# A two-layer transformer block on one Trainium2 core: first feed-forward halved, first products side by side, convolution taps as diagonal matrices on TensorE

## The chip, the core and the metric

The kernel runs on one core of one Trainium2 chip. The time is device microseconds of one execution, from its start to its end, the median of three runs. The engines are TensorE (PE, matmuls; PEld is its weight load, which overlaps them), VectorE (DVE), ScalarE (ACT), GpSimd (POOL) and SyncE (SP), whose queue issues the DMA transfers.

## The reference

Two layers work on 512 tokens x and 256 context tokens (768 rows together) of width 1024. Each layer is a feed-forward, a mixer and a feed-forward, each of them behind an RMS norm that is modulated by a conditioning vector. The even mixer joins latent attention with an mLSTM; the odd mixer is a short convolution with a gated linear recurrence. In the last layer only x is kept.

```python
def modulate(h, shift, scale):
    return h * (1.0 + scale) + shift

def swiglu(h, w_gate, w_up, w_down):            # 1024 -> 2816 -> 1024
    return (jax.nn.silu(h @ w_gate) * (h @ w_up)) @ w_down

def short_conv(u, w, b):                        # CONV_W = 4, two to the left, one to the right
    out = lax.conv_general_dilated(u, w[:, None, :].astype(u.dtype), window_strides=(1,),
                                   padding=[(CONV_PAD_L, CONV_PAD_R)],
                                   dimension_numbers=('NWC', 'WIO', 'NWC'),
                                   feature_group_count=u.shape[-1])
    return out + b

def odd_mixer(hx, hc, w_in, conv_w, conv_b, w_a, b_a, w_x, b_x, lam, w_out, need_ctx):
    gate_x, xr_x = jnp.split(hx @ w_in, 2, axis=-1)
...
    xc_x = short_conv(xr_x, conv_w, conv_b)
    xc_c = short_conv(xr_c, conv_w, conv_b)
...
    y_x = ((hf_x + jnp.flip(hb_x, 1)).astype(hx.dtype) * jax.nn.gelu(gate_x)) @ w_out

# reference, each layer
        x = x + FFN_RESIDUAL * mx[2] * swiglu(modulate(rms_norm(x, norm_g[layer, 0]), mx[0], mx[1]), ...)
...
            y_x, y_c = odd_mixer(hx, hc, ...)
        x = x + mx[5] * y_x
        x = x + FFN_RESIDUAL * mx[8] * swiglu(modulate(rms_norm(x, norm_g[layer, 2]), mx[6], mx[7]), ...)
```

## The kernel before

Activations lie transposed: eight chunks of 128 features (`xT[k]`), each with 768 columns, 256 of context (C) and 512 of x (X). Every factor is split into a high and a low part in a rounded fp32 format, and a product is three matmuls, high x high, low x high, high x low (`xh`, `xl`; weights in a `unit`). ACT casts the high part of a weight (L260), DVE takes the low part (L261). A product over 770 columns (768 and two that carry the shift of the modulation) is 48 matmuls of 258 and 512 columns in turn: eight chunks, three parts, two column ranges. Plain fp32 matmuls, which need no split, run as two passes.

The stages follow each other: start, first feed-forward (`gen_ffn`, plain), even mixer, second and third feed-forward (`gen_halved`), odd mixer, last feed-forward (`gen_halved`, x only). A feed-forward has 22 column blocks f; each takes a gate product and an up product (L598), and after a group of blocks (`HG` gives the group sizes) the down product over them (L782 plain, L908 halved). `gen_halved` computes its first `NP` blocks plainly; for the other blocks it uses a scheme of seven products over halves where the plain way has eight (L730), from sums of halves of the activations (made during the plain blocks) and of the weights (DVE, L239 to L248).

Between two stages stands a joint. As each chunk of the residual comes out of the last product, DVE adds it to `xT` (L741). `scale` then gives the chunk's `xh` (ACT, L551) and `xl` (DVE, L552), `square` its squares (ACT, L562) and their running sum `acc` (L563), which is on POOL for chunks below `SQ`. The next stage's first product takes the chunks in order. Its norm factor (`norm`: `ah`, `al`, two pairs of sums on PE, L584/L585 or L718/L719, then a reciprocal of 768 columns on DVE) is only needed when a product is scaled afterwards.

The modulation vectors are products of the conditioning vectors with large weights. For three vectors of layer 0, four steps each, PE does it (`order`; a step is `mod_load`, three loads by SP, `mod_mm`, 8 fp32 matmuls that show as 16 records, and `mod_post`; L366, L377); the others go to DVE as 'late' multiply-adds (`mod_late`, L465), spread over the stages by `fill` and `mod_some`. `MS["left"]` and `mod_ready` see to it that a group is there when it is used.

At the start X and C are transposed, the first eight modulation steps run, `scale` follows chunk by chunk, and `first` computes X's part of the gate product, then of the up product, then four more modulation steps, then C's parts (`part`, L611).

The odd mixer works on eight column blocks n. `values(n)` is a product (V) whose scaled form is Z (L634); `branch(n)` (B) a product over x alone; the convolution turns Z into U: POOL multiplies tap 2 and adds the bias (L1860), DVE adds two small edge terms (L1869) and the other three taps over both column ranges, six operations (L1873); then U is split into `uh` and `ul` (L1877 to L1880). `gates(n, d)` are 12 matmuls each (L1900), after which a recurrence runs on ACT and DVE (L1929 to L1936). `odd_order` writes V, B, gates and recurrences of several blocks in an interleaved order; a scheduler may reorder engines within blocks marked `ordered`.

## Time and profile before

| | us |
|---|---|
| median of three runs (2865.7 to 2867.91) | 2867.61 |
| the profiled execution | 2867.53 |
| its span, first to last instruction | 2865.8 |
| PE busy (96% of the span) | 2756.6 |
| DVE busy (78%) | 2229.0 |
| ACT busy (38%) | 1096.7 |
| POOL busy (9%) | 263.8 |
| granted PE clock, mean | 0.978 |

Busy times are unions of what the engine had in work; a busy PE may still run at the lower of its two clock levels, which the granted clock tells. Of the chain of waits that ended last, PE holds 54% and DVE 9%. Stages, in us from the start of the span: start to 72, first feed-forward to 622, even mixer to 1188, second feed-forward to 1718, third to 2248, odd mixer to 2492, last feed-forward to 2866.

### The profile page before, as it was taken

What the parts mean: (1) busy time and instruction counts of PE and PEld (TensorE: products, weight loads), DVE (VectorE), ACT (ScalarE), POOL (GpSimd) and SP (SyncE); (2) the same over time, 40 slices, a digit from 0 to 9 for tenths busy, and PEclk for the clock granted to TensorE, in tenths of its full rate; (3) what the DMA queues carried; (4) which work ended last, traced back from release to release, by engine and by line L of the source; (5) the groups of instructions that cost most, each with busy time, mean ns of one, the idle gap of its engine ahead of it and who ended that gap; (6) DMA issues with size and microseconds to landing.
All of it is one profiled execution on the core that took longest, in us unless ns stands there. A gap on an engine that the chain in (4) does not pass through costs nothing.

```text
span 2865.8 us, 40947 instructions
## 1 busy us (share of the span) xinstructions
PE 2756.6 (96%) x16185; PEld 2453.1 (86%) x16185; DVE 2229.0 (78%) x3673; ACT 1096.7 (38%) x1743; POOL 263.8 (9%) x274
## 2 busy tenths in 40 slices
PE   6999999999999899899999999999999997899998
PEld 4888888888888677789999998999999886799997
DVE  5367767796765667878879897989887899888886
ACT  4212111234443456443223344323323475643433
POOL 1000000021342200100000010000000353100000
PEclk8999999999999899999999999999999998899999
DMA  7434333342443110123223232234322211223332
GB/s 208 124 114 133 119 128 125 122 141 54 139 146 107 55 58 31 52 77 100 87 83 107 89 95 72 91 116 147 133 92 71 58 57 49 85 82 103 100 101 87
DMA packets 356634, 282.00 MB, mean 98 GB/s; under 512 B 14665, under 2 KB 327226, under 8 KB 356442
## 3 DMA queue, kind: packets, MB, share of 16 engines
q1 hardware_dynamic: 353722, 266.02, 30.1%
q0 software_dynamic: 2720, 13.37, 1.3%
q8 instruction: 127, 2.08, 0.3%
q14 instruction: 65, 0.53, 0.1%
HBM read 263.78 MB, written 15.56 MB: 97 GB/s over the span
## 4 chain that ended last, share of the span: by engine, by line
PE 54%; DVE 9%; issue 1%; ACT 1%; DMA 1%; POOL 0%; SPq 0%; DVEq 0%; ACTq 0%
PE ps L730 24%; PE ps L908 16%; PE ps L598 8%; PE ps L1416 2%; DVE xl L552 2%; DVE unit L261 1%; DVE xT L741 1%; PE oacc L1633 1%; PE ps L1590 1%; PE ps L1621 1%; DVE U L1873 1%; PE ps L1900 1%; DVE I L1931 0%; DVE S L1936 0%; DVE S L1929 0%
## 5 line engine op out<-in xcount | busy, mean ns | idle before, releaser
L598 PE MATMUL ps<-xh,unit 128*128 128x258 f32 (+3 forms) x3328 | 727.4, 337 | 10.5 <-DVE unit L261 8.7
L260 ACT CAST unit<-raw 128x1024 fp32r<-128x1024 f32 (+3 forms) x338 | 333.7, 988 | 943.7 <-PE ps L598 236.1
L598 PEld LDWEIGHTS ps<-xh,unit 128*128 128x128 f32 x3328 | 568.3, 193 | 77.8 <-DVE unit L261 10.1
L730 PE MATMUL ps<-xh,unit 128*128 128x386 f32 (+1 forms) x2592 | 617.6, 321 | 0.8 <-DVE g L804 0.7
L730 PEld LDWEIGHTS ps<-xh,unit 128*128 128x128 f32 x2592 | 451.6, 189 | 4.6 <-DVE g L804 1.5
L598 PE MATMUL ps<-xl,unit 128*128 128x258 f32 (+4 forms) x1664 | 425.6, 335 | 16.1 <-DVE xl L522 9.4
L261 DVE TENSOR_TENSOR unit<-raw,unit 128x1024 fp32r<-128x1024 f32 (+3 forms) x354 | 410.8, 1162 | 32.2 <-ACT unit L260 30.4
L908 PE MATMUL ps<-ah,unit 128*128 128x256 f32 (+1 forms) x1760 | 418.3, 349 | 2.5 <-ACT ah L521 2.5
L730 PE MATMUL ps<-xl,unit 128*128 128x386 f32 (+1 forms) x1296 | 414.1, 320 | 0.0
L598 PEld LDWEIGHTS ps<-xl,unit 128*128 128x128 f32 (+1 forms) x1664 | 311.1, 193 | 49.1 <-DVE xl L522 11.0
L908 PEld LDWEIGHTS ps<-ah,unit 128*128 128x128 f32 x1760 | 306.0, 188 | 48.6 <-ACT ah L521 4.5
L741 DVE SCALAR_TENSOR_TENSOR xT<-ps,mv,xT 128x256 f32<-128x256 f32 (+1 forms) x368 | 216.6, 633 | 74.3 <-PE ps L908 47.2
L908 PE MATMUL ps<-al,unit 128*128 128x256 f32 (+1 forms) x880 | 249.1, 349 | 0.0
L730 PEld LDWEIGHTS ps<-xl,unit 128*128 128x128 f32 x1296 | 244.7, 189 | 0.8
L465 DVE SCALAR_TENSOR_TENSOR macc<-mraw,csT,macc 128x768 f32<-128x768 f32 x245 | 241.0, 1017 | 2.0 <-DMA mraw<-in_mod_w_dram 1.9
L563 POOL TENSOR_TENSOR acc<-acc,sq 128x768 f32<-128x768 f32 (+1 forms) x33 | 65.2, 1975 | 1523.3 <-ACT sq L562 829.4
L908 PEld LDWEIGHTS ps<-al,unit 128*128 128x128 f32 x880 | 165.3, 188 | 23.4 <-DVE al L522 1.2
L626 DVE COPY bias<-ps 128x2 f32<-128x2 f32 (+1 forms) x82 | 12.7, 155 | 189.8 <-PE ps L598 186.5
L782 PE MATMUL ps<-ah,unit 128*128 128x256 f32 x704 | 152.8, 337 | 0.0
L782 PEld LDWEIGHTS ps<-ah,unit 128*128 128x128 f32 x704 | 120.1, 188 | 15.2
L521 ACT CAST ah<-u 128x768 fp32r<-128x768 f32 (+1 forms) x88 | 68.8, 782 | 112.5 <-DVE u L816 93.3
L730 PE MATMUL ps<-xh,four 128*128 128x386 f32 (+1 forms) x432 | 108.7, 320 | 0.0
(384 smaller groups left out, 3895.0 us busy)
## 6 DMA issues: line engine op xcount, KB each, us to landing
mraw<-in_mod_w_dram SPq DMA_DIRECT2D x184, 384.0 KB, 5.5
raw<-in_ffn_w_gate_dram SPq DMA_DIRECT2D x88, 512.0 KB, 3.9
raw<-in_ffn_w_up_dram SPq DMA_DIRECT2D x88, 512.0 KB, 3.9
raw<-in_ffn_w_down_dram SPq DMA_DIRECT2D x48, 512.0 KB, 3.6
raw<-in_ffn_w_down_dram SPq DMA_DIRECT2D x40, 384.0 KB, 3.2
raw<-in_even_w_in_dram SPq DMA_DIRECT2D x21, 512.0 KB, 5.1
raw<-in_odd_w_in_dram SPq DMA_DIRECT2D x16, 512.0 KB, 4.0
raw<-in_ffn_w_down_dram SPq DMA_DIRECT2D x16, 320.0 KB, 2.9
```

The costliest lines, as they stand in the source:

```text
L260: nc.scalar.copy(u[:, 0, 0:w], t)
L261: (nc.gpsimd if e == 2 else v).tensor_tensor(out=u[:, 1, 0:w], in0=t, in1=f(u[:, 0, 0:w]), op=ALU.subtract)
L465: v.scalar_tensor_tensor(out=o, in0=r[:, 0:768], scalar=s, in1=o, op0=ALU.mult, op1=ALU.add)
L521: nc.scalar.copy(hi, src)
L552: v.scalar_tensor_tensor(out=lo[:, a + o:b + o], in0=xT[k][:, a:b], scalar=s, in1=f(h[:, a + o:b + o]), op0=ALU.mult, op1=ALU.subtract)
L563: eng.tensor_tensor(out=self.acc[:, t], in0=self.acc[:, t], in1=sq[:, t], op=ALU.add)
L598: mm(ps[0:m, 0:b - a], lhsT=u[:, wi, k, 0:m], rhs=src[k][:, a:b], start=k == 0 and i == 0, stop=k == KD - 1 and i == 2)
L730: mm(ps[:, 0:H], lhsT=u[:, wi, o + k, :], rhs=src, start=start, stop=k == 3 and wi == 1, skip_group_check=True)
L741: v.scalar_tensor_tensor(out=xT[d][:, a:b], in0=ps[:, 0:b - a], scalar=mod_vec(l, n, d, j), in1=xT[d][:, a:b], op0=ALU.mult, op1=ALU.add)
L782: mm(ps[:, 0:b - a], lhsT=u[:, wi, q, :], rhs=src[:, a:b], start=q == 0 and i == 0, stop=q == G - 1 and i == 2)
L908: mm(ps[:, 0:c.stop - c.start], lhsT=us[n][:, wi, q, :], rhs=src[:, c], start=q == 0 and i == 0, stop=q == G - 1 and i == 2)
L1416: mm(ps[:, 0:b - a], lhsT=u[:, wi, q, o:o + 128], rhs=src[:, a:b], start=q == 0 and i == 0, stop=q == len(ys) - 1 and i == 2)
```

## The change

1. The first feed-forward becomes a `Halved` one with `NP0` = 4 plain blocks, as the second and third are (`add_halved(0, 0, NP0)`, `gen_halved`).
2. `order` takes twelve more modulation steps (vectors 6, 7 and 8 of layer 0, those of its last feed-forward) to PE. `fill` issues one at every second turn until 12 are done, then one in 14. The late list loses these vectors, 64 multiply-adds.
3. `together` computes two products by pairs of chunks in turn. It is used for gate and up of a feed-forward's first block and for V and B of the odd mixer's first block; `proj_start` does the like for the even mixer's gates and first v. X's parts in `first` alternate by chunk.
4. `SQ` = `SQ3` = 0: the running sum of squares is on DVE for all chunks. `HG` ends with a group of four. `proj_start` runs in the scheduler's order for DVE and ACT.
5. Start: X is scaled before C, the weights are split one step earlier, one more load is issued ahead, the norm comes after the modulation steps.
6. The convolution: POOL builds four diagonal matrices of taps a block, PE multiplies Z by them into PSUM, ACT adds the bias on the way out. The six DVE operations and POOL's two are gone; the edge terms stay.

```diff
-SQ = 8
+SQ = 0
-SQ3 = 6
+SQ3 = 0
-SPI = 5
+SPI = 4
+ML = 2
-PE0 = 1
+PE0 = 0
-MF0 = 6.3
+MF0 = 0.5
-HG = [4, 4, 4, 4, 3, 3]
+HG = [4, 4, 4, 3, 3, 4]
+NP0 = 4
+MP = 14
+FP = 1
...
-    order = [(0, 4 * n + i) for n in (1, 0, 2) for i in range(4)]
+    order = [(0, 4 * n + i) for n in (1, 0, 2, 7, 6, 8) for i in range(4)]
...
+        def together(self, us, tiles=(None, None)):
+            out = [[] for _ in us]
+            left = [self.product_steps(u, o, tiles=t) for u, o, t in zip(us, out, tiles)]
+            while left:
+                left = [g for g in left if next(g, g) is not g]
+            return out
...
-            if f == 0 and first is not None:
-                pg, pu = first
+            if f == 0:
+                pg, pu = first or P.together([ws.next(), ws.next()])
+                if first is None:
+                    P.norm()
+                yield
...
         def values(n):
-            pz = steps()
             if n == 0:
+                early.extend(P.together([ws.next(), ws.next()], (None, XO)))
                 P.norm()
+            pz = steps() if n else early[0]
...
-            for a, b, s in P.spans():
-                nc.gpsimd.tensor_scalar(out=U[n][:, a:b], in0=Z[:, a:b], scalar1=vec("conv_w", 16 + n, 1), scalar2=cb[:, s, 0:1],
-                                        op0=ALU.mult, op1=ALU.add)
-            UH[n] = Z, eb
+            dg = slot(name="dg")
+            for j in range(4):
+                nc.gpsimd.tensor_scalar_mul(dg[:, 128 * j:128 * j + 128], ident, vec("conv_w", 8 * j + n, 1))
+            UH[n] = Z, cb, eb, dg
 
         def conv(n):
...
+            pss = [bank() for _ in SEGS]
+            for j, lo, hi, sh in ((2, 0, 0, 0), (1, 1, 0, -1), (0, 2, 0, -2), (3, 0, 1, 1)):
+                for ps, (a, b) in zip(pss, SEGS):
+                    mm(ps[:, lo:b - a - hi], lhsT=dg[:, 128 * j:128 * j + 128], rhs=Z[:, a + lo + sh:b - hi + sh],
+                       start=j == 2, stop=j == 3, skip_group_check=True)
+            for ps, (a, b), s in zip(pss, SEGS, (C, X)):
+                act(out=U[n][:, a:b], in_=ps[:, 0:b - a], func=ACTF.Identity, bias=cb[:, s, 0:1])
...
-            for a, b in SEGS:
-                for j, lo, hi, sh in ((1, 1, 0, -1), (0, 2, 0, -2), (3, 0, 1, 1)):
-                    o = U[n][:, a + lo:b - hi]
-                    v.scalar_tensor_tensor(out=o, in0=Z[:, a + lo + sh:b - hi + sh], scalar=cw(j), in1=o,
-                                           op0=ALU.mult, op1=ALU.add)
...
-    run(gen_ffn(P[0], 0, 0, P[1].chunk, pss), fill)
+    run(gen_halved(P[0], 0, 0, P[1].chunk, pss, NP0), fill)
```

PE at the head of the odd mixer, before: the end of V of block 0 (L598), the norm's sums over `ah` and `al` (L584, L585), and the next products.

```order
L598 MATMUL ps<-xh,unit 128x258
L598 MATMUL ps<-xh,unit 128x512
L584 MATMUL nps<-ah,ones 128x384 x2
L598 MATMUL ps<-xh,unit 128x258
L598 MATMUL ps<-xh,unit 128x256
L598 MATMUL ps<-xl,unit 128x258
L585 MATMUL nps<-al,ones 128x384 x2
L598 MATMUL ps<-xl,unit 128x256
L598 MATMUL ps<-xh,unit 128x258
L598 MATMUL ps<-xh,unit 128x256
```

The same place after: the norm's sums (L593, L594), then block 0's convolution (Z against its diagonal matrices `dg`, L1903), then a product again (L607).

```order
L594 MATMUL nps<-al,ones 128x384
L593 MATMUL nps<-ah,ones 128x384
L594 MATMUL nps<-al,ones 128x384
L1903 MATMUL ps<-Z,dg 128x256
L1903 MATMUL ps<-Z,dg 128x512
L1903 MATMUL ps<-Z,dg 128x255
L1903 MATMUL ps<-Z,dg 128x511
L1903 MATMUL ps<-Z,dg 128x254
L1903 MATMUL ps<-Z,dg 128x510
L1903 MATMUL ps<-Z,dg 128x255
L1903 MATMUL ps<-Z,dg 128x511
L607 MATMUL ps<-xh,unit 128x258
```

Eight diagonal matmuls stand between the norm's sums and the next product, which followed at once before.

DVE at the joint from the even mixer to the second feed-forward, before: residuals (`xT`, L741) and low parts (`xl`, L552) of chunks 2 to 5.

```order
L741 SCALAR_TENSOR_TENSOR xT_74<-ps,mv_96,xT_74 128x512
L552 SCALAR_TENSOR_TENSOR xl<-xT_74,mv_96,xh 128x256
L741 SCALAR_TENSOR_TENSOR xT_75<-ps,mv_96,xT_75 128x256
L552 SCALAR_TENSOR_TENSOR xl<-xT_74,mv_96,xh 128x512
L741 SCALAR_TENSOR_TENSOR xT_75<-ps,mv_96,xT_75 128x512
L552 SCALAR_TENSOR_TENSOR xl<-xT_75,mv_96,xh 128x256
L741 SCALAR_TENSOR_TENSOR xT_76<-ps,mv_96,xT_76 128x256
L261 TENSOR_TENSOR unit<-raw,unit 128x1024
```

The same after (L764, L561), with the running sum of squares (L572).

```order
L764 SCALAR_TENSOR_TENSOR xT_74<-ps,mv_96,xT_74 128x512
L572 TENSOR_TENSOR acc<-acc,sq 128x768
L561 SCALAR_TENSOR_TENSOR xl<-xT_74,mv_96,xh 128x256
L561 SCALAR_TENSOR_TENSOR xl<-xT_74,mv_96,xh 128x512
L764 SCALAR_TENSOR_TENSOR xT_75<-ps,mv_96,xT_75 128x256
L764 SCALAR_TENSOR_TENSOR xT_75<-ps,mv_96,xT_75 128x512
L572 TENSOR_TENSOR acc<-acc,sq 128x768
L561 SCALAR_TENSOR_TENSOR xl<-xT_75,mv_96,xh 128x256
L561 SCALAR_TENSOR_TENSOR xl<-xT_75,mv_96,xh 128x512
L572 TENSOR_TENSOR acc<-acc,sq 128x768
```

The sums now stand in DVE's row between the low parts, one a chunk; a residual moved behind them.

## Rows read from the trace of the kernel before

**Rows 1.** Stages by windows: PE, PEld, DVE, ACT, POOL busy us (instructions), PEclk, DMA share, GB/s.

```profile
0.00:72.00 72.00, 48.35 (x292) 31.16 (x293) 42.74 (x87) 29.44 (x53) 9.22 (x21) 0.86 0.71 207
72.00:622.00 550.00, 549.13 (x3217) 476.50 (x3216) 372.24 (x550) 123.41 (x170) 10.27 (x5) 1.00 0.39 125
622.00:1188.00 566.00, 536.31 (x3060) 448.09 (x3058) 388.15 (x945) 266.71 (x597) 121.51 (x166) 0.96 0.28 85
1188.00:1718.00 530.00, 523.31 (x2986) 489.63 (x2987) 452.29 (x657) 186.15 (x256) 14.18 (x9) 0.99 0.28 89
...
2248.00:2492.00 244.00, 212.18 (x1158) 183.41 (x1157) 218.62 (x303) 155.06 (x211) 87.88 (x57) 0.92 0.21 61
2492.00:2866.00 374.00, 361.08 (x2462) 332.54 (x2460) 304.56 (x487) 152.91 (x206) 3.98 (x4) 0.99 0.31 94
```

**Rows 2.** Chain of waits in the second feed-forward: start us, us, what; then PE's timeline.

```profile
1206.02 59.27 PE ps L598 x336
...
1718.61 0.51 PE L598 MATMUL ps<-xh,unit 128*128 128x260 f32 x2
```

**Rows 3.** PE timeline of the first feed-forward, one modulation step and what follows.

```profile
109.25 1.07 PE L366 MATMUL mps<-mraw,csT 128*32 128x256 f32 x16
...
110.44 0.60 PE L598 MATMUL ps<-xh,unit 128*128 128x258 f32 x2
```

**Rows 4.** PE timeline of the start, its three longest idle times (in brackets).

```profile
36.40 0.80 PE L611 MATMUL ps<-xh,unit 128*128 128x512 f32 x1 [2.95 <-ACT unit L260]
...
40.36 1.22 PE L611 MATMUL ps<-xh,unit 128*128 128x512 f32 x2 [2.74 <-DVE unit L261]
...
50.88 0.49 PE L611 MATMUL ps<-xh,unit 128*128 128x512 f32 x1 [3.43 <-ACT xh L551]
```

**Rows 5.** PE timeline at the joints between stages, the idle times.

```profile
626.74 1.55 PE L598 MATMUL ps<-xh,unit 128*64 128x258 f32 x4 [3.17 <-DVE unit L261]
...
668.10 1.93 PE L1137 MATMUL ps<-ident,zv 128*128 128x128 f32 x6 [4.40 <-ACT zv L1175]
...
1199.00 0.58 PE L598 MATMUL ps<-xl,unit 128*128 128x260 f32 x1 [6.29 <-DVE xl L522]
...
1729.01 0.79 PE L598 MATMUL ps<-xl,unit 128*128 128x512 f32 x1 [2.81 <-DVE xl L552]
...
2498.21 0.80 PE L598 MATMUL ps<-xl,unit 128*128 128x258 f32 x2 [3.83 <-DVE xl L552]
```

**Rows 6.** Line L552 by source: ns min/median/max; then groups by form: busy us, mean ns.

```profile
L552 DVE SCALAR_TENSOR_TENSOR xl<-xT,mv,xh x88: 469/743/2344, 30.3 to 2501.5; 128x512 fp32r<-128x512 f32 x48, 128x256 fp32r<-128x256 f32 x40
...
L563 POOL TENSOR_TENSOR acc<-acc,sq 128x768 f32<-128x768 f32 x28 | 57.1, 2039 | 1477.9 <-ACT sq L562 784.3 <-ACT xh L521 690.3 <-ACT xh L551 2.5
...
L563 DVE TENSOR_TENSOR acc<-acc,sq 128x768 f32<-128x768 f32 x7 | 6.6, 948 | 0.1
```

**Rows 7.** Five odd-mixer column blocks as one window (columns as in rows 1); group L1873.

```profile
2298.80:2416.10 117.30, 101.63 (x611) 90.86 (x610) 109.99 (x145) 79.60 (x103) 54.55 (x34) 0.93 0.18 51
...
L1873 DVE SCALAR_TENSOR_TENSOR U<-Z,vecT,U 128x255 f32<-128x255 f32 (+3 forms) x48 | 32.9, 738 | 0.2
```

**Rows 8.** Plain fp32 matmuls: PE timeline of the even mixer, then their group by form.

```profile
866.37 1.03 PE L1265 MATMUL num<-W,unv 128*128 128x256 f32 x4
...
L1265 PE MATMUL num<-W,unv 128*128 128x256 f32 x192 | 51.1, 381 | 2.0 <-DVE W L1251 1.9
```

**Rows 9.** Odd mixer, timelines: norm's last sum, Z, a late gate product; chain: two gate products.

```profile
2264.56 1.01 PE L585 MATMUL nps<-al,ones 128*128 128x384 f32 x2 [1.09 <-DVE al L522]
...
2275.97 1.02 DVE L634 TENSOR_TENSOR Z<-ps,ry 128x256 f32<-128x256 f32 x2
...
2343.55 0.77 PE L1900 MATMUL ps<-uh,unit 128*128 128x512 f32 x1 [4.34 <-DVE G L634]
...
2286.27 4.22 PE ps L1900 x24
...
2343.55 3.97 PE ps L1900 x11
```

More of the change, by code (lines that the diff above doesn't have):

```diff
@@ L46 @@
 OM = ''
+OE = 'DVE,Activation'
+OEN = 0
 OA = ''
@@ L411, in mod_late @@
     def mod_late():
-        todo = [(l, g, b, k) for l, g in ((0, 1), (0, 2), (1, 0), (1, 1), (1, 2)) for b in range(4) for k in range(KD)]
+        todo = [(l, g, b, k) for l, g in ((0, 1), (1, 0), (1, 1), (1, 2)) for b in range(4) for k in range(KD)]
         raw, tail = {}, []
@@ L539, in chunk, with scale @@
             self.square(k, v if k >= (SQ3 if self.l and self.n == 2 else SQ) else nc.gpsimd)
-        def scale(self, k, pool=False):
+        def scale(self, k, pool=False, only=None):
             l, n = self.l, self.n
-            h, lo = slot(F32R, "xh"), slot(F32R, "xl")
-            self.h[k], self.lo[k] = h, lo
+            if self.h[k] is None:
+                self.h[k], self.lo[k] = slot(F32R, "xh"), slot(F32R, "xl")
+            h, lo = self.h[k], self.lo[k]
             for a, b, j in self.segs:
+                if only not in (None, j):
+                    continue
                 o = self.off[j]
@@ L706, in settle, with parts @@
             self.t1 = None
-        def norm(self):
+        def parts(self):
             ah, al = slot(F32R, "ah"), slot(F32R, "al")
@@ L711, in norm @@
             split_to(ah[:, t], al[:, t], self.acc[:, t])
+            self.acc = ah, al
+        def norm(self):
+            if not isinstance(self.acc, tuple):
+                self.parts()
+            ah, al = self.acc
             w = self.nt // 2
@@ L827, in whole @@
                 yield
-                if f == 0:
-                    P.norm()
                 pu = P.product(ws.next())
@@ L1112, in proj_start @@
     def proj_start(P):
-        pss = P.product(ws.next(), 64)
+        pss = []
+        gates = P.product_steps(ws.next(), pss, 64)
         M["z"], M["turn"] = {}, [[], []]
         first = gen_proj(P, [("v", 0)])
-        next(first)
+        for _ in range(3):
+            next(gates)
+            next(first)
+        run(gates)
         P.norm()
@@ L1711, in project @@
             run(gen_proj(P, keys))
-        z, rows = proj_start(P)
-        M["turn"][-1].append((rope_keys, z))
-        next(rows)
+        with ordered(OE):
+            z, rows = proj_start(P)
+            M["turn"][-1].append((rope_keys, z))
+            next(rows)
         for n, key in enumerate([("c", i) for i in range(5)] + [("q", 0), ("k", 0), ("o", 0)]):
-            project(key)
+            with ordered(OE if n < OEN else ""):
+                project(key)
             if n == 5:
@@ L1883, in branch @@
         def branch(n):
-            pg = steps(XO)
+            pg = steps(XO) if n else early[1]
             bg = P.bias(pg, tiles=XO)
@@ L2005, in tile_hybrid_block @@
             ws.preload(PL)
+    ws.preload(1)
     MS["load"] = 8
-    P = [Normed(0, 0), Normed(0, 1), Halved(0, 2), Halved(1, 0), Normed(1, 1), Halved(1, 2, True)]
+    P = [Halved(0, 0), Normed(0, 1), Halved(0, 2), Halved(1, 0), Normed(1, 1), Halved(1, 2, True)]
     def start():
@@ L2035, in start @@
                 for k in (2 * i - 4, 2 * i - 3):
-                    P[0].scale(k, PE0)
+                    P[0].scale(k, only=X)
+        P[0].parts()
+        for k in range(KD):
+            P[0].scale(k, PE0, C)
     def first():
         us, pss = [ws.next(False) for _ in range(2)], [[bank() for _ in ALL] for _ in range(2)]
-        P[0].part(us[0], pss[0][1], 1)
-        if NI:
-            P[0].norm()
-        P[0].part(us[1], pss[1][1], 1)
-        if not NI:
-            P[0].norm()
+        a, b, _, _ = P[0].tiles[1]
+        for k in range(KD):
+            for u, ps in zip(us, pss):
+                for i, (wi, src) in enumerate(((0, P[0].h), (0, P[0].lo), (1, P[0].h))):
+                    mm(ps[1][:, 0:b - a], lhsT=u[:, wi, k, :], rhs=src[k][:, a:b], start=k == 0 and i == 0,
+                       stop=k == KD - 1 and i == 2)
         for n in range(4, 9):
@@ L2051, in first @@
                 mod_post(n - 1)
+        for n in range(8, 8 + ML):
+            mod_load(n)
+        MS["load"] = 8 + ML
         P[0].shifts()
+        ws.presplit(1)
+        P[0].norm()
         for i in range(2):
@@ L2058, in fill @@
     def fill():
-        MS["n"] = MS.get("n", 0) + 1
-        if MS["n"] < FS:
-            pass
-        elif MS["mm"] <= len(order):
-            mod_step(FL)
-        else:
+        n = MS["n"] = MS.get("n", 0) + 1
+        if n < FS:
+            pass
+        elif MS["posted"] < 12:
+            if n % 2 == FP:
+                mod_step(FL)
+        else:
+            if n % MP == 0:
+                mod_step(1)
             some_late()
```

11 lines of the change are left out of this document (6 added, 5 removed).

## The prediction

> **What bounds the kernel now.** I read the windows by stage first [rows 1]. In the two full-width feed-forwards shown, TensorE (PE) is busy for nearly the whole stage: 549 of 550 us in the first, 523 of 530 in the second, both at a granted clock of 0.99 or more, that is, at the upper of its two levels (2.4 GHz). There time goes only with matmuls. Three places differ: the start (48 of 72 us busy, clock 0.86), the even mixer and the odd mixer. In the odd mixer PE is busy 212 of 244 us, while VectorE (DVE) is busy 219; inside five of its column blocks DVE has 110.0 of 117.3 us, PE 101.6 [rows 7]. So DVE sets the pace there, 23.5 us a block, and PE waits at the joints.
>
> The second view is the chain of waits, for prices. One stretch of 336 matmuls of a gate/up product takes 59.27 us, 0.1764 us each [rows 2], a mean over 258 and 512 columns, so 0.353 us for a pair of 770 columns. A gate product of the odd mixer, 24 matmuls, takes 4.22 us at that pace [rows 9]. Third, PE's timeline at the joints: waits of 2.8 to 6.3 us, mostly for DVE's low parts xl [rows 5]. A wait also leaves something behind: after 4.34 us of idle time 11 gate matmuls took 3.97 us, where 24 take 4.22 [rows 9]; 11 should take 1.94. That is half pace, PE's lower level (1.2 GHz), and costs 2.0 us more. I price a joint at its wait plus 2.
>
> **The change part by part.** The sum is made against the profiled run, 2867.5 us, 2865.8 of span and 1.7 around it; that is 0.1 below the median of the three runs.
>
> *First feed-forward halved.* Before: 550 us. After, its first four column blocks are plain and the other 18 take 84 matmuls in place of 96, as the second feed-forward already has it: 2112 gate/up matmuls become 384 + 1512. 96 of the 384 lie in the start as before; 288 remain, 288 x 0.1764 = 50.8 us. The part behind the plain blocks is what the second feed-forward spends from 1206.02 + 59.27 = 1265.29 to 1718.61 [rows 2], 453.3 us. The 16 modulation steps that now stand in this stage (4 before) cost PE 1.19 us each, from the first of one to the next product [rows 3]: 19.0. Sum 523.1, so **-27**. The 12 additional steps take the place of 64 late DVE multiply-adds. They bring 36 loads into SyncE's queue among the weights, but the same bytes went through that queue later, and the DMA share is 0.39 in this stage [rows 1]. I take the loads at nothing; if a slot holds the queue, weights come late. The nearest row for a late weight at PE is 3.43 us once [rows 4], or below nothing, since later stages lose those loads: -3 to +4.
>
> *Start.* The gate product waits three times, 2.95 + 2.74 + 3.43 = 9.1 us [rows 4], as chunks and weights arrive. Gate and up side by side give PE six matmuls a chunk in place of three, and the weights are split one step earlier. But both weights must be ready before the second matmul group. Between -4 and -11; I take **-8**, nearest to the sum of the waits.
>
> *Joints.* Side by side, a chunk pair feeds 24 matmuls, 4.2 us, where 12 gave 2.1; a new last group of four blocks lengthens the product before. What speaks against it: the running sum of squares goes from GpSimd (POOL), 2.04 us each, to DVE, 0.95 us each [rows 6]. Seven a joint put 6.6 us into just the chain that PE waits for. In return xl (line L552) should no longer be stretched: its median is 0.743 us, its longest 2.344 [rows 6]. Sixteen of them stand at a joint; if about four are stretched by 1.6 us each, that is 6.4 us, so I take DVE's chain as unchanged, between -6.4 and +6.6. The cover then decides: with gate and up side by side PE has 8.5 us more work that needs no later chunk, longer than any wait there. Wait plus 2 us: first feed-forward to even mixer 3.17 + 2 = **-5**; even mixer to second feed-forward 6.29 + 2 = **-8**; second to third 2.81 + 2 = **-5**; odd mixer to last 3.83 + 2 = **-6** [rows 5]. The 4.40 us wait behind the gates [rows 5] stays: some 90 matmuls stand before it then as now.
>
> The trace shows the stretch at the joints while POOL sums; the Trainium skill, "SBUF — State Buffer", section "SBUF: two separate sides", says why: a DVE operation with two SBUF inputs and a POOL operation that reads SBUF share one pair of ports, and whichever comes first blocks the other. The trace agrees as far as it goes, 2.344 against 0.743 us. By the rule the joints' four terms stand as above, -24; without it the squares come on top and the sum is that of the second rival below, 2848.
>
> *Odd mixer.* The convolution becomes eight plain fp32 matmuls a block, over 768 + 766 + 764 + 766 = 3064 columns, two passes each. A pass of 256 columns: four took 1.03 us, one alone shows 0.381, so the spacing is (1.03 - 0.381)/3 = 0.216 [rows 8]. 3064/256 x 2 x 0.216 = 5.2 us a block, 41.4 in all. DVE loses 32.9/8 = 4.1 us a block [rows 7], 22.0 - 4.1 = 17.9. PE's work: eight value products (48 matmuls) at 8.5, eight branch products by columns (512 of 770, with some fixed part) at 5.9, eight pairs of gates at 4.2, out product 192 x 512 columns 45, norm 1: 195 us. With the convolution 236. PE then needs 23.8 us a block, as much as DVE paced before. On top, waits. The order puts convolution 0 right behind the norm and ahead of block 1's products, which filled that time before. PE waits from the norm's last sum at 2264.56 + 1.01 until Z is there at 2275.97 + 1.02 [rows 9]: 11.4 us, or 11 with one weight split less; then 2 us at half pace. Z of each further block stands on DVE behind recurrence work: 0.5 us x 6 = 3, an estimate, between 0 and 4.3 each [the wait of rows 9]. Ends 4. 236 + 11 + 2 + 3 + 4 = 256, against 244: **+12**, between -4 and +30.
>
> That PE holds its order is seen in the 4.40 us wait [rows 5]: independent products stood behind. The Trainium skill, "TensorE: Matmul & The Clock Gate", section "The mechanism" of Part 3, says matmuls never overtake each other; by the opposite, the 11 + 2 us would fall to nothing and the time by 13.
>
> Sum: -27 - 8 - 5 - 8 - 5 - 6 + 12 = -47. 2867.5 - 47 = **2820 us**.
>
> **The rivals.** *Odd mixer at par*: if Z comes without waits and DVE's shorter work shows at the ends too, the +12 becomes about -2: 2806. For it: DVE no longer bounds. Against: convolution 0 is plainly exposed.
> *Joints stay*: xl stays as slow as it is, the squares' 6.6 us lengthen DVE's chain as much as the doubled cover gives back, and the start gains half: 24 + 4 us do not come, 2848. For it: seven sums more on the engine named in most waits.
> *Lockstep in the odd mixer, slower than before*: every convolution on PE waits for Z, Z stands on DVE behind sums whose inputs come from gates that PE has just done. If the two alternate rather than overlap, each of six blocks costs up to 17.9 us more, 107 in all: 2927. It turns the sign once more than 47/6 = 7.8 us a block are exposed. Against it: the products of one block, 8.5 and 5.9 us, lie between a block's gates and its use.
> *It does not do what it says*: the order shows the fewer matmuls, so this has next to no chance.
>
> **How the numbers follow.** Forecast 0.52, odd mixer at par 0.20, joints stay 0.20, lockstep 0.05, others 0.03. The range reaches to both middle rivals and a few us beyond for the loads and the Z waits: 2797 to 2849. Measurable is 0.2%, 5.7 us. Faster by more: 0.94; within: 0.02; slower: 0.04, nearly all lockstep.
>
> **What would show it.** The first feed-forward's stage at 519 to 527 us with PE busy throughout; a wait of about 11 us on PE ahead of the first diagonal matmuls, and those at some 5.2 us a block; odd blocks at 24 us with DVE at three quarters; L563's successor on DVE at 0.95 us; joint waits under 2 us. The forecast is wrong if PE waits for weight splits in the first feed-forward, if joints still show waits of 3 us or more, or if Z's wait recurs at each block.

## The result

| | before | after |
|---|---|---|
| median, us (4 runs each) | 2866.65 | 2820.89 |
| ratio, 95% interval | | 0.9844 [0.9827, 0.9861] |
| span of the profiled execution, us | 2865.8 | 2817.3 |
| PE busy, us (share of the span) | 2756.6 (96%) | 2751.1 (98%) |
| granted PE clock, mean | 0.978 | 0.988 |

The kernel became 1.6% faster; 2820 us was forecast. By stages of the two profiled executions, with bounds at the start of each stage's first product in PE's timeline:

| stage | before | after | difference | forecast |
|---|---|---|---|---|
| start | 72.4 | 60.7 | -11.7 | -8 |
| first feed-forward | 550.3 | 527.6 | -22.7 | -27 |
| even mixer | 564.5 | 557.9 | -6.6 | -5 |
| second feed-forward | 531.4 | 522.3 | -9.1 | -8 |
| third feed-forward | 529.6 | 523.8 | -5.8 | -5 |
| odd mixer | 244.0 | 256.0 | +12.0 | +12 |
| last feed-forward | 373.6 | 369.0 | -4.6 | -6 |
| sum | 2865.8 | 2817.3 | -48.5 | -47 |

The windows of the kernel after by these bounds, to be laid beside [rows 1] (same columns):

```profile
0.00:60.70 60.70, 45.74 (x297) 30.39 (x298) 32.43 (x79) 30.84 (x60) 1.80 (x14) 0.92 0.94 280
60.70:588.30 527.60, 527.07 (x3178) 483.22 (x3177) 455.74 (x700) 181.06 (x258) 2.15 (x3) 1.00 0.39 122
588.30:1146.20 557.90, 532.77 (x3056) 446.80 (x3055) 373.70 (x934) 266.93 (x599) 111.23 (x159) 0.97 0.27 83
1146.20:1668.50 522.30, 522.30 (x2991) 489.22 (x2990) 450.02 (x667) 187.23 (x260) 0.11 (x1) 1.00 0.29 91
1668.50:2192.30 523.80, 523.34 (x3015) 489.61 (x3014) 461.84 (x673) 182.29 (x250) 1.73 (x6) 1.00 0.34 110
2192.30:2448.30 256.00, 239.52 (x1293) 197.51 (x1292) 181.62 (x262) 161.57 (x223) 80.46 (x67) 0.97 0.20 58
2448.30:2817.30 369.00, 360.35 (x2461) 331.42 (x2460) 303.45 (x490) 153.23 (x207) 0.00 (x0) 1.00 0.32 95
```

PE has no idle time in the second feed-forward and half a microsecond in the first and third, and the clock is at its upper level there. In the odd mixer PE is still idle for 16 of 256 us, most of it at one place. PE's timeline shows what is left of the waits of [rows 4, 5, 9] (idle time in brackets):

```profile
35.35 0.72 PE L2084 MATMUL ps<-xh,unit 128*128 128x512 f32 x1 [2.42 <-ACT unit L266]
...
627.58 1.92 PE L1165 MATMUL ps<-ident,zv 128*128 128x128 f32 x6 [4.46 <-ACT zv L1203]
...
2218.11 8.01 PE L1903 MATMUL ps<-Z,dg 128*128 128x256 f32 x16 [10.66 <-DVE Z L651]
...
2240.32 5.31 PE L1903 MATMUL ps<-Z,dg 128*128 128x256 f32 x16
...
2381.08 5.42 PE L1903 MATMUL ps<-Z,dg 128*128 128x256 f32 x16 [2.18 <-POOL dg L1894]
```

The start waits 2.42 us once, where it waited 2.95, 2.74 and 3.43. The wait behind the even mixer's gates is what it was, 4.46 us. The joints have vanished from the list but for 1.07 us at the last. Block 0's convolution waits 10.66 us for Z, and its 16 records take 8.01 us where those of block 1 take 5.31: the first eight stand twice as far apart as the others, that is, they run at half pace. The last block's waits 2.18 us for its diagonal matrices from POOL.

Five blocks of the odd mixer (compare [rows 7]):

```profile
2250.00:2368.30 118.30, 118.30 (x681) 99.70 (x680) 87.31 (x114) 83.65 (x112) 54.86 (x43) 1.00 0.18 52
```

PE is busy for all of 118.3 us, 23.66 a block, and DVE for 87.3, where PE had 101.6 and DVE 110.0 of 117.3. The bound went from one engine to the other at nearly the same pace.

The low parts at the joints, by source (min/median/max ns), and the sums of squares by form, both to be read against [rows 6]:

```profile
L561 DVE SCALAR_TENSOR_TENSOR xl<-xT,mv,xh x88: 474/741/754, 30.2 to 2456.1; 128x512 fp32r<-128x512 f32 x48, 128x256 fp32r<-128x256 f32 x40
```

```profile
L572 DVE TENSOR_TENSOR acc<-acc,sq 128x768 f32<-128x768 f32 x35 | 33.3, 951 | 0.1
```

The longest low part is 0.754 us, not 2.344: nothing stretches it any more. The rows by form give what that is worth (busy us, mean ns), before and after:

```profile
L552 DVE SCALAR_TENSOR_TENSOR xl<-xT,mv,xh 128x512 fp32r<-128x512 f32 x48 | 54.8, 1141 | 8.0 <-ACT xh L551 8.0
...
L552 DVE SCALAR_TENSOR_TENSOR xl<-xT,mv,xh 128x256 fp32r<-128x256 f32 x40 | 33.2, 830 | 0.0
```

```profile
L561 DVE SCALAR_TENSOR_TENSOR xl<-xT,mv,xh 128x512 fp32r<-128x512 f32 x48 | 35.4, 747 | 1.8 <-ACT xh L560 1.3
...
L561 DVE SCALAR_TENSOR_TENSOR xl<-xT,mv,xh 128x256 fp32r<-128x256 f32 x40 | 18.6, 480 | 0.0
```

By the means, 48 x 0.394 + 40 x 0.350 = 33 us are saved over all low parts, and 28 sums at 0.951 us bring 27 us to DVE.

### The profile page after: what moved, and what is told of

The parts are those of the page before. It is cut to its first block, busy times and chain, and to the rows that moved or that the text cites. A ratio compares the mean times of both kernels' runs of the same rounds, so it can differ in the third digit from the quotient of the medians.

```text
span 2817.3 us, 41304 instructions
## 1 busy us (share of the span) xinstructions
PE 2751.1 (98%) x16283; PEld 2468.2 (88%) x16283; DVE 2258.8 (80%) x3800; ACT 1163.1 (41%) x1853; POOL 197.5 (7%) x250
## 4 chain that ended last, share of the span: by engine, by line
PE 91%; DVE 4%; ACT 2%; DMA 1%; issue 1%; SPq 1%; POOL 0%; DVEq 0%; ACTq 0%; POOLq 0%
PE ps L753 35%; PE ps L932 24%; PE ps L607 18%; PE ps L1444 2%; PE ps L1903 2%; PE num L1293 1%; PE ps L1618 1%; PE oacc L1661 1%; PE ps L1649 1%; PE ps L1270 1%; PE ps L1935 1%; PE mps L372 1%; PE ps L1532 1%; PE ps L1568 1%; DVE unit L267 1%
## 5 line engine op out<-in xcount | busy, mean ns | idle before, releaser
L753 PE MATMUL ps<-xh,unit 128*128 128x386 f32 (+1 forms) x3456 | 847.2, 326 | 0.6 <-DVE g L827 0.5
L753 PEld LDWEIGHTS ps<-xh,unit 128*128 128x128 f32 x3456 | 610.4, 189 | 4.2 <-DVE g L827 1.5
L932 PE MATMUL ps<-ah,unit 128*128 128x512 f32 (+1 forms) x2464 | 573.4, 346 | 2.5 <-ACT ah L527 2.5
L753 PE MATMUL ps<-xl,unit 128*128 128x386 f32 (+1 forms) x1728 | 561.0, 325 | 0.0
L932 PEld LDWEIGHTS ps<-ah,unit 128*128 128x128 f32 x2464 | 426.5, 188 | 63.6 <-ACT ah L527 4.5
L607 PE MATMUL ps<-xh,unit 128*128 128x258 f32 (+5 forms) x2176 | 469.8, 331 | 1.1 <-ACT xh L560 1.1
L607 PEld LDWEIGHTS ps<-xh,unit 128*128 128x128 f32 (+1 forms) x2176 | 362.7, 189 | 43.1 <-issue 2.3
L753 PEld LDWEIGHTS ps<-xl,unit 128*128 128x128 f32 x1728 | 326.4, 189 | 1.2
L764 DVE SCALAR_TENSOR_TENSOR xT<-ps,mv,xT 128x512 f32<-128x512 f32 (+1 forms) x400 | 233.3, 632 | 74.5 <-PE ps L932 58.7
L607 PE MATMUL ps<-xl,unit 128*128 128x258 f32 (+2 forms) x1088 | 273.1, 326 | 0.0
L607 PEld LDWEIGHTS ps<-xl,unit 128*128 128x128 f32 x1088 | 198.5, 189 | 18.6
L827 DVE TENSOR_TENSOR u<-ps,u 128x386 f32<-128x386 f32 (+1 forms) x216 | 112.4, 520 | 39.3 <-PE ps L753 38.8
## 6 DMA issues: line engine op xcount, KB each, us to landing
mraw<-in_mod_w_dram SPq DMA_DIRECT2D x24, 256.0 KB, 6.0
```

The costliest lines, as they stand in the source:

```text
L607: mm(ps[0:m, 0:b - a], lhsT=u[:, wi, k, 0:m], rhs=src[k][:, a:b], start=k == 0 and i == 0, stop=k == KD - 1 and i == 2)
L753: mm(ps[:, 0:H], lhsT=u[:, wi, o + k, :], rhs=src, start=start, stop=k == 3 and wi == 1, skip_group_check=True)
L764: v.scalar_tensor_tensor(out=xT[d][:, a:b], in0=ps[:, 0:b - a], scalar=mod_vec(l, n, d, j), in1=xT[d][:, a:b], op0=ALU.mult, op1=ALU.add)
L827: v.tensor_tensor(out=out, in0=ps[:, 0:H], in1=more, op=ALU.add)
L932: mm(ps[:, 0:c.stop - c.start], lhsT=us[n][:, wi, q, :], rhs=src[:, c], start=q == 0 and i == 0, stop=q == G - 1 and i == 2)
```

## The experiments

Twelve kernels ran, four on a chip at a time, each beside the kernel before. Its median there was 2866.68, 2866.65 and 2869.55 us, so times of the last four (e8 to e11) are read by their difference from it; the changed kernel has -45.8. The diffs below are shortened (`...`), and of `OB0` and `OB1` they show only the value in use. No run takes back by itself the halving of the first feed-forward, the order at the start, the change of `HG` or that of `proj_start`; what these are worth is read from the stages alone.

### e1: block 0's convolution behind V1 and B1

```diff
-OB0 = "V0 B0 C0 V1 B1 C1"
+OB0 = "V0 B0 V1 B1 C0 C1"
```

> Block 0's convolution is moved behind block 1's V and B products, nothing else. In the changed kernel PE waits 10.66 us ahead of it. Theory (PE works in its order, and the wait is exposed only because nothing independent stands before the convolution): the 14.4 us of V1 and B1 cover the wait; the odd stage falls from 256.0 to about 243 us (10.7 of wait and 2 to 3 of half pace), the whole to about 2808. Rival (the wait only moves, for example to V1 or B1, because the PSUM banks held for Z0 and G0 come free only after Z0): a wait of 5 to 10 us shows within V1 and B1, and the stage stays at 250 us or more.

2809.59 us, ratio 0.9798 [0.9783, 0.9814], 11 us less than after: the first expectation. The odd stage as a window, and the two convolutions on PE:

```profile
2194.60:2437.10 242.50, 236.73 (x1293) 196.31 (x1292) 181.18 (x262) 161.49 (x223) 80.53 (x67) 1.00 0.21 61
```

```profile
2223.97 10.45 PE L1903 MATMUL ps<-Z,dg 128*128 128x256 f32 x32
```

The stage falls to 242.5 us. The 32 records of both convolutions follow without idle time, 10.45 us, at full pace. The wait was exposed because PE keeps its row; with independent products ahead of it, it costs nothing.

### e2: twelve modulation steps back on DVE

```diff
-    order = [(0, 4 * n + i) for n in (1, 0, 2, 7, 6, 8) for i in range(4)]
+    order = [(0, 4 * n + i) for n in (1, 0, 2) for i in range(4)]
...
-        todo = [... for l, g in ((0, 1), (1, 0), (1, 1), (1, 2)) ...]
+        todo = [... for l, g in ((0, 1), (0, 2), (1, 0), (1, 1), (1, 2)) ...]
...
-MF0 = 0.5
+MF0 = 0.8
-MF2 = 0.52
+MF2 = 0.56
```

> The twelve modulation steps that the change gave to PE go back to DVE's late multiply-adds (the rate of late work in the first feed-forward set so that they are done before the joint to the second). Theory: the halved first feed-forward leaves DVE no room for them. DVE is busy 456 of 528 us there; about 56 multiply-adds at 1.0 us and their folds make some 530, over the 511 us that PE would need (528 less 12 steps of 1.4 us). The stage becomes DVE-bound, 535 to 550 us, and the whole 2827 to 2845. Rival (PE alone sets the stage): it falls to 511 us and the whole to 2804.

2824.09 us, ratio 0.9848 [0.9833, 0.9863]: the same as after within the intervals. Neither expectation held. The first feed-forward, and two waits of PE:

```profile
61.90:582.60 520.70, 514.66 (x2978) 477.94 (x2977) 486.68 (x711) 175.67 (x245) 2.14 (x3) 1.00 0.36 116
```

```profile
453.88 0.57 PE L753 MATMUL ps<-xh,unit 128*128 128x386 f32 x1 [2.52 <-DVE g L827]
...
1130.04 0.30 PE L447 MATMUL mps<-fold,quart 128*32 128x12 f32 x8 [3.12 <-DVE fold L439]
```

The stage falls by 6.9 us to 520.7, though 12 steps of 1.4 us left PE. DVE rises to 487 of 521 us, and PE waits for it at three places, 2.52 us the longest. What the stage wins goes back later: the even mixer takes 5.9 us more and the second feed-forward 3.2, each with a wait of PE for a fold of late work that was not done in time (3.12 and 1.79 us). Only 101 multiply-adds ran in the stage, so the rest had moved on. The steps cost PE 17 us, and DVE had no free place for all of them.

### e3: the convolution back on POOL and DVE

```diff
-    pss = [bank() for _ in SEGS]  ... mm(..., lhsT=dg[...], rhs=Z[...]) ... act(out=U[n][:, a:b], ...)
+    nc.gpsimd.tensor_scalar(out=U[n][:, a:b], in0=Z[:, a:b], ...)        # in values(n)
+    v.scalar_tensor_tensor(out=o, in0=Z[:, a + lo + sh:b - hi + sh], scalar=cw(j), in1=o, ...)   # three taps
```

> The convolution alone goes back to POOL (one tap and the bias) and DVE (three taps), the rest of the change stays, block 0's order too. Theory: the diagonal matmuls cost PE 41 us and win nothing that PE can use, since DVE's 23.5 us a block is what PE needs with them; block 0's wait is exposed only with them. The odd stage falls from 256.0 to 240 to 246 us, the whole to 2804 to 2811. Rival (DVE's bound was worse than its pace: waits of 4 to 5 us between blocks and half clock come back on top): 250 to 260 us, the whole within 6 us of 2820.

2805.5 us, ratio 0.978 [0.9763, 0.9797], 15 us less than after. The odd stage, and three of its waits:

```profile
2190.80:2429.10 238.30, 207.71 (x1165) 179.84 (x1164) 214.01 (x310) 152.81 (x207) 78.48 (x51) 0.94 0.21 62
```

```profile
2282.83 0.77 PE L1934 MATMUL ps<-uh,unit 128*128 128x512 f32 x1 [4.34 <-DVE G L651]
...
2319.75 0.63 PE L607 MATMUL ps<-xh,unit 128*128 128x258 f32 x2 [3.60 <-DVE unit L267]
...
2372.40 1.01 PE L1934 MATMUL ps<-ul,unit 128*128 128x256 f32 x2 [5.51 <-DVE ul L1914]
```

238.3 us against 256.0, and the whole is as the first expectation has it. PE has 208 us of work and waits again, at five places 3.6 to 5.5 us each, four times for DVE and once for ACT, and the clock falls to 0.94. That is cheaper than 41 us of diagonal matmuls with no wait between blocks. By itself the convolution on TensorE is a loss here: 11 us of it are block 0's place (e1); the other 4 are less certain, as the two intervals overlap.

### e4: the sums of squares back on POOL

```diff
-SQ = 0
+SQ = 8
-SQ3 = 0
+SQ3 = 6
```

> The running sums of squares go back to POOL (SQ = 8, SQ3 = 6), the products stay side by side. Theory (the doubled cover closed the joints, the place of the sums is nearly neutral): the four joints open by 0 to 2 us each, the whole 2819 to 2828. Rival (POOL's sums stretch DVE's low parts, and their removal closed the joints): waits of 3 to 6 us are back at each joint, the whole 2832 to 2845.

2834.06 us, ratio 0.9882 [0.9866, 0.9899], 13 us more than after. The sum is in the rival's range, but a wait of over 3 us at the head of a stage is back at one joint only. The second feed-forward rises by 8.3 us to 530.6, the odd mixer by 2.7, the last by 3.2; the third does not (523.9). PE, DVE and POOL at the joint to the second feed-forward, then the low parts and the residuals by source:

```profile
1160.70 0.59 PE L607 MATMUL ps<-xl,unit 128*128 128x260 f32 x1 [6.03 <-DVE xl L528]
```

```profile
1158.46 4.10 POOL L572 TENSOR_TENSOR acc<-acc,sq 128x768 f32<-128x768 f32 x2 [2.84 <-ACT sq L571]
...
1158.85 3.73 DVE L528 TENSOR_TENSOR xl<-mv,xh 128x4 fp32r<-128x4 f32 x5
```

```profile
L561 DVE SCALAR_TENSOR_TENSOR xl<-xT,mv,xh x88: 468/745/2406, 30.4 to 2471.3; 128x512 fp32r<-128x512 f32 x48, 128x256 fp32r<-128x256 f32 x40
...
L764 DVE SCALAR_TENSOR_TENSOR xT<-ps,mv,xT x400: 440/739/751, 125.9 to 2827.9; 128x512 f32<-128x512 f32 x78, 128x256 f32<-128x256 f32 x56
```

The same place in the kernel after, on DVE and on PE:

```profile
1156.47 0.59 DVE L528 TENSOR_TENSOR xl<-mv,xh 128x4 fp32r<-128x4 f32 x7
...
1157.55 0.28 PE L607 MATMUL ps<-xl,unit 128*128 128x260 f32 x1
```

Low parts take up to 2.406 us again. Of the five operations on four columns two take 1.79 us, each beside a sum of POOL, and three 0.15, while seven take 0.59 us together in the kernel after. The residuals (L764), which read one input from PSUM, are not stretched: 0.751 us at most, with POOL's sums beside them.

The stretch is not the whole of this wait. Without it the first small operation would have ended 1.64 us earlier (1.79 less 0.15), and PE waits 6.03. In this run, as counted in the trace, PE comes to the matmul that needs it after 22 of the pair's 96 matmuls (20 in the kernel before), 5.8 us into the stage; in the kernel after 53 stand ahead of it in PE's row, and PE comes to it 11.4 us into the stage, when the operand is ready. At the joint to the third feed-forward six low parts take over 2 us each in this run, and that stage does not rise at all. So the edit changed the scheduler's order on PE as well, and no run separates this order from the stretch.

### e5: the first products one by one

```diff
             left = [self.product_steps(u, o, tiles=t) for u, o, t in zip(us, out, tiles)]
-            while left:
-                left = [g for g in left if next(g, g) is not g]
+            for g in left:
+                for _ in g:
+                    pass
```

> The two products at the head of the second, third and last feed-forward and of the odd mixer run one after the other again (the second product starts when the first is done; the norm stays behind both); the sums of squares stay on DVE. In the changed kernel the last low part comes 10.9 us after the even mixer's joint to the second feed-forward begins, 6.7 us after the next, 7.2 us at the odd mixer and 9.5 us at the last feed-forward; a single first product covers 8.5, 8.5, 8.5 and 5.8 us. Theory (with low parts no longer stretched only what outlasts the first product is exposed, plus 2 us of half pace): 4.5 + 0 + 0 + 5.7, about 10 us, the whole 2827 to 2834. Rival (the doubled cover is what closed all joints): waits of 3 to 6 us at all four, the whole 2838 to 2848.

2821.12 us, ratio 0.9841 [0.9825, 0.9858]: no difference, against both. The second feed-forward:

```profile
1146.80:1669.20 522.40, 522.40 (x2992) 489.24 (x2991) 450.54 (x668) 187.24 (x260) 0.11 (x1) 1.00 0.29 91
```

No idle time. PE's row tells why, as far as parts and widths of its matmuls show: after 20 matmuls of the gate product the scheduler put two of the up product, and so on in turn; 53 stand ahead of the first that needs a late small low part, as in the kernel after. The scheduler fills waits of one product with the other by itself, as long as nothing stands between them. The edit therefore did not give the order that its expectation speaks of.

### e10: the norm between the two products

```diff
-            if f == 0:
-                pg, pu = first or P.together([ws.next(), ws.next()])
-                if first is None:
-                    P.norm()
+            if f == 0 and first is not None:
+                pg, pu = first
                 yield
             else:
                 pg = P.product(ws.next())
                 yield
+                if f == 0:
+                    P.norm()
                 pu = P.product(ws.next())
```

> In the changed kernel the norm's sums of a feed-forward's first block go back between its gate and up product (as in the kernel before); the sums of squares stay on DVE; the odd mixer is left as it is. Theory (with the sums on DVE the low parts come early enough; the pair of products matters only where they do not): the joint to the second feed-forward, where the last low part comes 10.9 us after the joint begins, opens by 2 to 4 us, the others by 0 to 2; the whole 2822 to 2828. Rival (the place of the norm behind both products closed the joints): waits of 3 us or more at each of the three, the whole 2830 to 2840.

2832.83 us, ratio 0.987 [0.9855, 0.9885], -36.7 from the kernel before on its chip, so 9 us of the gain are lost. PE's row is again 48 gate matmuls, the norm's six sums, 48 up matmuls, and 28 matmuls stand ahead of the first that needs a late small low part. The head of the second and of the last feed-forward:

```profile
1144.80:1170.00 25.20, 22.46 (x109) 18.45 (x109) 21.64 (x32) 12.17 (x20) 0.00 (x0) 0.86 0.21 61
2455.70:2480.00 24.30, 21.39 (x152) 20.49 (x151) 21.59 (x36) 12.76 (x20) 0.00 (x0) 0.86 0.30 87
```

The longest of PE's waits at the first of them:

```profile
1151.07 0.50 PE L607 MATMUL ps<-xh,unit 128*128 128x512 f32 x1 [1.41 <-ACT xh L560]
```

The second feed-forward rises by 6.7 us to 529.0, the last by 4.7, the third not at all; the odd mixer, which the edit leaves as it is, by 2.7, and why was not traced. The places are those of the first expectation, but the sum lies in the rival's range (2830 to 2840), whose waits of 3 us at each of the three joints did not come. The waits are small, 1.41, 0.28, 0.68 and 0.38 us at the first joint. But the clock is 0.86 over these 25 us, so half pace costs more than the waits.

### e8: the kernel before, sums of squares on DVE

```diff
-SQ = 8
+SQ = 0
-SQ3 = 6
+SQ3 = 0
```

> The kernel before, with one edit: the running sums of squares on DVE for all chunks (SQ = 0, SQ3 = 0). The changed kernel keeps all its joints closed when the first products run one by one, and opens them when the sums go back to POOL. Theory (the place of the sums alone closes the joints, since DVE's low parts are no longer stretched): even mixer to second feed-forward -8, to third -6, odd mixer -3, last -4, together about -20; the whole 2842 to 2850 against 2866.7. Rival (the norm behind both products is needed too): waits of 2 to 4 us stay at the joints, since PE's row has the norm's sums between the two products; the whole 2852 to 2862.

2857.18 us, ratio 0.9957 [0.9943, 0.9971]: 12 us of the 46. That is in the rival's range, also when it is read by the difference from the kernel before. Second feed-forward -4.1 us, third -4.8, odd mixer -4.3, but even mixer +2.6 and last +0.5. DVE and PE at the joint to the even mixer, and PE at that to the second feed-forward:

```profile
633.89 3.80 DVE L465 SCALAR_TENSOR_TENSOR macc<-mraw,csT,macc 128x768 f32<-128x768 f32 x4
...
638.68 0.44 PE L598 MATMUL ps<-xl,unit 128*64 128x258 f32 x1 [2.24 <-DVE xl L522]
...
1195.63 0.49 PE L598 MATMUL ps<-xh,unit 128*128 128x512 f32 x1 [1.40 <-ACT xh L551]
...
1197.84 0.50 PE L598 MATMUL ps<-xh,unit 128*128 128x512 f32 x1 [0.69 <-ACT xh L551]
```

Where one wait of 6.29 us was, several small ones remain, 1.40, 0.69 and others. At the even mixer there is a new one of 2.24 us: DVE's row has four late multiply-adds, 3.80 us, ahead of the small low parts that PE waits for. By this run and e10 both are needed, the sums off POOL and the norm behind both products.

### e7: both undone

> Both undone: the sums of squares on POOL and the first products one after the other. Theory (either cure closes the joint between second and third feed-forward, where the run with the sums on POOL showed no wait; the others need both): that joint opens by 5 to 6 us here and only here; even mixer to second feed-forward +9, odd mixer +3 to +6, last +5 to +6; the whole 2842 to 2850. Rival (the two act on separate joints and simply add): no wait at the second-to-third joint, the whole 2838 to 2842.

The edits of e4 and e5 together: 2840.69 us, ratio 0.991 [0.9895, 0.9924]. Since e5's edit leaves the order to the scheduler, this is not quite the joints of before. The joint to the third feed-forward opens:

```profile
1687.63 0.50 PE L607 MATMUL ps<-xl,unit 128*128 128x512 f32 x1 [2.06 <-DVE xl L561]
...
1690.33 1.01 PE L607 MATMUL ps<-xl,unit 128*128 128x260 f32 x2 [1.49 <-DVE xl L528]
```

That stage is 530.6 us, 6.8 more than after, while e4 alone had 523.9 there. The pairing written out matters at this joint, and only while POOL does the sums. This is the place that the first expectation names, and where the rival has no wait; the sum, 2840.69, is 1 us below the first expectation's range and within the rival's (2838 to 2842).

### e6, e6b: the convolution shared between PE and DVE

```diff
+CP = (1, 3, 5, 7)          # e6b: (2, 4, 6)
...
+            if n in CP:    # diagonal matrices and PE, as after
+            else:          # POOL and DVE, as before
```

> The convolution of blocks 1, 3, 5 and 7 stays on PE, that of blocks 0, 2, 4 and 6 goes back to POOL and DVE. Theory (the odd mixer is bound by whichever of PE and DVE has more, 23.7 us with all on PE, 23.5 with none): shared, PE has 18.6 and 23.7 in turn, 21.2 on average, DVE 17.5 and 21.6; block 0's exposed wait is gone. The stage falls below both, to 222 to 230 us, the whole to 2787 to 2796. Rival (each engine's waits for the other, not its load, set the pace): 238 to 245 us, the whole 2803 to 2810.

> As the run with blocks 1, 3, 5, 7, but blocks 2, 4 and 6 are on PE and 0, 1, 3, 5, 7 on POOL and DVE. Theory: PE has one convolution less, 5 us, but the last block's three taps stand in DVE's chain at the end of the mixer, 4 us: 222 to 230 us for the stage, the whole 2786 to 2797. Rival: as there.

2803.07 us, ratio 0.9776 [0.9762, 0.9791], and 2806.36, ratio 0.9789 [0.9774, 0.9804]. Odd stages of 236.7 and 242.1 us: the rival, though e6 lies 1.3 us below the range that it gives for the stage. The stage of e6, two of its convolutions on PE, and block 0's taps on DVE:

```profile
2195.00:2431.70 236.70, 221.31 (x1230) 186.07 (x1230) 198.65 (x287) 156.05 (x215) 83.22 (x59) 0.98 0.21 63
```

```profile
2229.97 7.20 PE L1912 MATMUL ps<-Z,dg 128*128 128x256 f32 x16 [5.44 <-DVE Z L652]
...
2272.76 5.55 PE L1912 MATMUL ps<-Z,dg 128*128 128x256 f32 x16 [1.41 <-DVE Z L652]
```

```profile
2223.76 3.83 DVE L1922 SCALAR_TENSOR_TENSOR U<-Z,vecT,U 128x255 f32<-128x255 f32 x6
```

PE has 221 us of work, DVE 199, in 237; neither is full. Z1 comes 5.44 us late for PE, since DVE does block 0's taps first, and each later Z 1.4 to 1.8 us. e6 is the fastest kernel of all, though its interval overlaps that of e3.

### e9, e11: convolutions behind B

```diff
-OB0 = "V0 B0 C0 V1 B1 C1"
+OB0 = "V0 B0 V1 B1 C0"
-OB1 = [""] + [f"C{n + 1} B{n + 1}" for n in range(1, 7)] + [""]
+OB1 = ["C1"] + [f"B{n + 1} C{n + 1}" for n in range(1, 7)] + [""]
```

> As the run with the convolution of blocks 1, 3, 5, 7 on PE, and PE's order changed: block 0's convolution behind V1 and B1, block 1's behind the first gates, each further one behind B of its block instead of ahead of it. There PE waited 5.4 us for Z1 and 1.4 to 1.8 us for each of Z3, Z5, Z7, with half pace behind. Theory (the waits for Z were what kept the shared convolution from its 21.2 us a block): about 10 of them and some 5 of half pace go; the odd stage falls from 236.6 to 220 to 227 us, the whole to 2786 to 2794. Rival (DVE is the next bound: its recurrence work fills the stage and the gates now wait for U and ul): waits of 2 to 4 us ahead of gates, the stage 230 to 238 us, the whole 2796 to 2804.

> All eight convolutions on PE as in the changed kernel, with PE's order of the run e9. Theory (PE then has no wait for Z and is bound by its work alone, 236 us, and 4 of ends): the odd stage 239 to 243 us, about that of the run with block 0's convolution moved alone (242.5), the whole 2806 to 2812. Rival (a convolution just ahead of a gate pair makes the gates wait for ACT's bias and the split): 0.5 to 2 us a block come back, the stage 245 to 255 us, the whole 2812 to 2822.

The diff is that of e11; e9 has `CP = (1, 3, 5, 7)` of e6 beside it. e9 (shared): 2825.47 us, ratio 0.9848 [0.9834, 0.9863], some 20 us worse than e6 (-44.1 against -63.6 from before) where 10 better were expected; its odd stage is 259.4 us. e11 (all on PE): 2810.24, ratio 0.9792 [0.9778, 0.9807], 13.5 us better than after by the differences from before. Two waits of e9 on PE, and DVE's timeline ahead of the second:

```profile
2233.65 1.22 PE L1949 MATMUL ps<-uh,unit 128*128 128x256 f32 x3 [6.58 <-ACT uh L1926]
...
2296.51 0.51 PE L608 MATMUL ps<-xh,unit 128*128 128x512 f32 x1 [4.14 <-DVE G L652]
```

```profile
2283.28 1.83 DVE L1978 SCALAR_TENSOR_TENSOR S<-R,S 128x768 f32<-128x768 f32 x2 [4.95 <-ACT S L1970]
...
2296.04 0.42 DVE L652 TENSOR_TENSOR G<-ps,ry 128x256 f32<-128x256 f32 x1
```

DVE stands 4.95 us in its row until ACT has done the recurrence's square root, then works 13 us on the recurrence and on weight splits, and the scaling of B (G) stands behind all that. PE's next product is released by G and waits 4.14 us, and as long once more a block later. The gates' wait of 6.58 us ends with block 0's split, which waits for block 0's taps on DVE; scalings of block 0 and block 1 stand ahead of these. So PE waits for a place in DVE's row, which neither expectation named; these three waits are about half of PE's 29 us of idle time, and the rest was not traced. With all convolutions on PE they don't arise, and the odd stage is

```profile
2194.10:2439.60 245.50, 239.77 (x1293) 198.07 (x1292) 177.50 (x263) 161.78 (x223) 85.69 (x67) 0.99 0.21 61
```

245.5 us with 1.96 us of wait for block 0's split. The stage is 2.5 us above the first expectation and at the lower end of the rival's range; the whole is within the first's. Against e1 the stage is 3 us longer, but the whole 2 us shorter when both are read from the kernel before (-59.3 and -57.1), so these runs do not rank the two orders.

## Why the prediction was right, step by step

The forecast was met within 1 us, and part of that is luck: the first feed-forward gained 4.3 us less than forecast, the start 3.7 more, and the joints closed for a reason that the prediction had only in part.

**The first feed-forward** (-22.7, forecast -27, within its +4). Once the steps are taken off, the halving came out as summed. The mis-sized term is the modulation step. The prediction took from the step's first row to the next product's, 1.19 us. PE's timeline of the kernel after shows one whole step:

```profile
105.05 0.52 PE L607 MATMUL ps<-xh,unit 128*128 128x260 f32 x2
105.50 1.07 PE L372 MATMUL mps<-mraw,csT 128*32 128x256 f32 x16
106.50 0.44 PE L383 MATMUL mps<-ident,msb 128*128 128x128 f32 x2
106.69 0.60 PE L607 MATMUL ps<-xh,unit 128*128 128x260 f32 x2
107.14 0.51 PE L607 MATMUL ps<-xl,unit 128*128 128x260 f32 x2
```

The pair of matmuls before starts at 105.05, the second pair behind at 107.14. Without a step, two pairs take 0.70 us, so a step costs 2.09 - 0.70 = 1.39 us; the prediction had missed 0.1 us at either side. Sixteen times 0.2 is 3.2 of the 4.3 us. Of the rest, 0.5 us is PE's idle time in the stage (527.60 less 527.07); the remainder was not traced. That the loads of the twelve steps cost nothing held: no wait for a weight stands in the stage.

**The start** (-11.7, forecast -8, just beyond its bound of -11). The three waits went from 9.1 to 2.4 us, PE's whole idle time from 23.7 to 15.0 (the windows less PE's busy time). The term left out half pace: the clock rose from 0.86 to 0.92 in the window, and PE's busy time fell from 48.4 to 45.7 us.

**The joints** (-26 over four, forecast -24): right in sum, in part for another reason. The prediction took DVE's chain as unchanged and let the pair of products cover the waits. Both of its sizes hold: the stretch was 33 us over all low parts, 6.6 a joint where it had 6.4, and the sums put nearly as much back. What it lacked is small: the two small operations of 1.79 us at the joint to the second feed-forward. What closed the joints is what stands in PE's row ahead of the late low parts. The pairing as written is worth nothing once DVE has the sums (e5). With the norm behind both products, and the sums on DVE, the scheduler puts 53 matmuls ahead of the first that needs the late ones at the joint to the second feed-forward; with the norm between the products 28 (e10, 9 us lost), with the sums on POOL 22 (e4, 13 us lost), in the kernel before 20. The sums' move is worth 12 us on the kernel before (e8) and 20 where the products are written one after the other (e7 against e5), so its worth depends on the rest; how much of it is the end of the stretch and how much the order on PE stays open. The second rival, joints stay, fell with its condition that low parts stay slow.

The rule cited from the Trainium skill ("SBUF — State Buffer", section "SBUF: two separate sides") is borne out: without POOL's sums 0.754 us is the longest low part, with them 2.406, and the residuals, with one input in PSUM, keep 0.751.

**The odd mixer** (+12.0, forecast +12). The convolution was summed at 5.2 us a block; the rows show 5.31, the last record's tail included. The exposed wait was 10.66 us, forecast 11, and half pace behind it cost 2.7 (8.01 less 5.31), forecast 2. PE's work without that is 236.8 us (239.52 less 2.7), forecast 236. The waits for Z in each block, 3 us, did not come; 2.18 us for the last diagonal matrices came unforeseen, and the rest of the idle time, mostly at the out product, is 3.6 us where the ends were put at 4. So the size is right with a small exchange between terms. e1 shows the wait by itself, 13.5 us of the stage with its half pace.

**The rivals.** Odd mixer at par is what e1 reaches by one order. Lockstep did not occur in the changed kernel: DVE has 6 us of slack a block. The nearest to it is e9, where an order alone cost 20 us.

**What stays open**: about half a microsecond in the first feed-forward; what the order on PE and the end of the stretch are worth each; and how e6's two engines could be made to overlap fully, for the one order tried for it was worse.
